# Splitting the work behind the second norm's transposes into three parts, and interleaving the output projection's halves more tightly, in an inference step on one core

## The chip, the cores and the metric

The program runs on one core of one Trainium2 chip. TensorE (PE, with its weight loads shown apart as PEld), VectorE (DVE), ScalarE (ACT), GpSimd (POOL) and SyncE (SP) each have an instruction queue of their own, which they work off in order; semaphores make one engine wait for another. The metric is the device time of one execution in microseconds (us), as the median of several runs. Before the change it is 2565.86 us, the median of 3 runs from 2562.7 to 2570.66.

## The reference

One decoder layer is applied to a prompt of 2048 positions and, with the same weights, to 8 samples of 4 positions (32 rows). All data are fp32, the model width is 1024. Cut to what matters here:

```python
def _layer_prompt(x, ...):
    q, k, v, u, vg = _project(x, norm1_g, w_in)          # RMSNorm, one projection
    ...                                                  # dilated attention -> att, gating unit -> u * gate
    x = x + jnp.concatenate([att, u * gate], axis=-1) @ w_out
    x = x + _swiglu(x, norm2_g, w_gate, w_up, w_down)

def _swiglu(x, g, w_gate, w_up, w_down):                 # D_FF = 2816
    h = _rmsnorm(x, g)
    return (jax.nn.silu(h @ w_gate) * (h @ w_up)) @ w_down
```

The change concerns the stretch from `@ w_out` to the first products with `w_gate` and `w_up`.

## The kernel before

Every fp32 operand of a matmul is split into a high part (rounded to TensorE's fp32r type) and a low part, the rest; a product is then three matmuls: high by high, high by low, low by high. Splitting is therefore a large part of the work beside TensorE: ACT makes the high part by a copy, and DVE or POOL subtracts it from the value to give the low part (`split_sb`, whose two instructions stand on lines 134 and 137 wherever it is called).

The 2048 positions are 16 token tiles of 128. The second half of the program works through them in three blocks: tiles 0 to 5, 6 to 11, and 12 to 15 together with the 32 sample rows. Within a block the tiles are numbered from 0; in the last block the sample rows are number 4. Each block has an opening, and then the SwiGLU, which takes the hidden width in 22 steps of 128 columns (f = 0 to 21).

The opening. The output projection of a tile is made in two halves of 512 columns: an "open" unit for the first half (`o0`, `o1`, ... in the table of the order) and a "second" unit for the second half (`s0`, `s1`, ...). A unit consists of two half units of 12 matmuls. After each half the result in PSUM is added to the residual in SBUF (L1364); the squares for the second norm are summed on ACT, half by half (L1385, L1391) or for the whole row (L1398); then comes the chain of the norm: L1373 and L1374 on DVE, a square root on ACT (L1375), four tiny DVE steps that refine the reciprocal root (L141 to L145), and L1406, which writes the normed tile xn (a buffer named pair; xns for the sample rows). `norm2_c` transposes xn by 8 matmuls on TensorE (L1420) into two PSUM tiles (ps_t). From those, three ACT copies (L1435, L1436, L1438) and six DVE subtractions (the low parts L1437 and L1440, and the four differences L1428 to L1431) give the operands of a Winograd product: seven products instead of eight stand for a two by two block product. The differences t1 to t4 lie in two buffers named zn and are split in two calls of `split_sb`, with the high parts on ACT and the low parts on POOL. Below, T0 to T5 are the transposes of tiles 0 to 5, and Ts those of the sample rows.

The SwiGLU's first step. For f = 0 the block's tiles are taken in two units, unit 0 (tiles 0 to 3; in the last block tiles 0 and 1) and unit 1 (the other two tiles), so that the first products can begin before all tiles are normed. A unit has seven products, q0 to q6, each 12 matmuls (L1552 to L1554) whose moving side is 256 columns wide in unit 0 of the first two blocks, 128 in their unit 1, and 136 in both units of the last block, where the sample rows are dealt out over the units. q0 needs the high and low part of the first transposed block (the low part is L1437's), q1 needs the difference t2, split by ACT and POOL. The later steps take the whole block at once (384 columns wide, 272 in the last block).

What sets the order. No scheduler decides it: the program issues the instructions in the order in which the Python code runs, and each engine has its own of them in that order. `tick()` is called once for each half unit or product, and `later(n, fn)` has fn run n ticks later. So the emission of the small work is spread by hand over the units of TensorE. The tables are in `next_block`: the string `work` orders the units, t says at which tick each first half is closed (`first_end`), and the last argument of `second_end`, put_off, says how many ticks after L1406 the tile is transposed.

In blocks 1 and 2 the opening begins while the block before is still ending: its last down products run on TensorE, and `finals` puts the final norm of each of its tiles (L1653 on ACT, L1374, L1375, L141 to L145, L1661 on DVE) in between. The loading and splitting of the second half of w_out falls there too: `half1_split` takes its eight slices two at a time into buffers named woh and wol, with the low parts on DVE or POOL. In the first block alone the even slices' low parts are DVE's. Slices of the activations are split by L1344 (ACT) and L1345 (DVE). Combined sources of the weights (`sources`) are loaded, summed and split on ACT and on DVE or POOL (L1492, L1496).

Of the kernel before, what the change touches and what calls it, by code (L numbers as in the profile page):

```python
# [64 lines left out]
def hymba_step(ctx: ExitStack, tc: tile.TileContext, A: dict, O: dict):  # L65
# [1336 lines left out]
    def norm2_b(B, i, s1, put_off):  # L1402
        n = B.rows[i]
        r = rms_c(s1, n)
        xn = square_tile() if n == P else B.xns
        dve.scalar_tensor_tensor(xn[:n], B.acc[i][:n], r, gain[1][:n], op0=OP.mult, op1=OP.mult)  # L1406
        if n == P:

            later(put_off, norm2_c, B, i, xn)

    def norm2_c(B, i, xn):
# [12 lines left out]
        (t1, t2), (t3, t4) = ((s_[:, 0], s_[:, 1]) for s_ in sums)  # L1424

        def sums_of():
# [4 lines left out]
            dve.tensor_sub(t4, b21, t2)  # L1431

        if n == P:
            at_ = lambda x, j0, j1: x[:, i, j0:j1, :, 0:64]
            act.activation(at_(hi, 0, 1)[:, 0], b11, AF.Copy)  # L1435
            act.activation(t4, b12, AF.Copy)  # L1436
            dve.tensor_sub(at_(lo_, 0, 1)[:, 0], b11, at_(hi, 0, 1)[:, 0].bitcast(F32))  # L1437
            act.activation(at_(hi, 1, 3), pts[1], AF.Copy)  # L1438
            sums_of()
            dve.tensor_sub(at_(lo_, 1, 3), pts[1], at_(hi, 1, 3).bitcast(F32))  # L1440
            for s_, j in zip(sums, (3, 5)):
                split_sb(at_(hi, j, j + 2), at_(lo_, j, j + 2), s_)
        else:
            act.activation(t4, b12, AF.Copy)
            sums_of()
            for j, x in enumerate((b11, b21, b22, t1, t2, t3, t4)):
                at_ = lambda y: y[:, :, j, :, 64:].rearrange("p i k c -> p k i c")
                x = x.rearrange("p k (i c) -> p k i c", i=B.nt)
                split_sb(at_(hi), at_(lo_), x, eng_lo=dve)
# [333 lines left out]
    def first_block(B):  # L1783
# [45 lines left out]
    def next_block(B, downs, finals):  # L1829
# [28 lines left out]
        for part in work.split():  # L1858
            i = int(part[1])
            if part[0] == "s":  # L1860
                second_end(B, i, second_unit(B, i), (2, 2, 2, 2, 1, 2)[i] if not B.last else (2, 2, 1, 3, 2)[i])
# [4 lines left out]
            if B.last and i == 3:  # L1866
# [186 lines left out]
```

## Time and profile before

| what | value |
|---|---|
| time, median of 3 runs | 2565.86 us (2562.7 to 2570.66) |
| the profiled execution | 2577.92 us, span 2576.1 us |
| mean granted TensorE clock in it | 0.978 |
| busy: PE, DVE, ACT, POOL | 2482.0, 1332.2, 1011.4, 1310.3 us |
| the opening of block 0 around its transposes | about 940 to 996 us |
| the opening of block 1 | about 1499 to 1590 us |
| the opening of the last block | about 2090 to 2151 us |
| f = 0 of the last block | about 2151 to 2192 us |

The profiled execution took 12 us longer than the median of the timed ones, and every duration that is read from the trace belongs to it. Times in the trace count from the start of the span. A row of the timeline gives start and duration in us, the engine, the line, the operation, output and inputs with their shape, and in brackets how long the engine had been idle and which instruction's end released it. A row of the waits says which line of an engine waited for what: us in total, times, and the longest. A row of the windows gives for a stretch its length, each engine's busy time with its instructions in parentheses, the granted clock of TensorE as a share of full speed (PEclk), and the DMA engines' load.

### The profile page before, as it was taken

How to read it: one execution, taken by the hardware profiler on the slowest of the kernel's cores; microseconds unless marked ns; L12 is line 12 of the kernel's file. 1: busy time of each engine (PE TensorE's matmuls, PEld its weight loads, DVE VectorE, ACT ScalarE, POOL GpSimd, SP SyncE). 2: the span in 40 equal slices, each digit the busy share in tenths (PEclk: the TensorE clock that was granted, in tenths of full speed). 3: DMA queues.
4: the chain of work that ended last, by engine and by line, in shares of the span. 5: the costliest groups of instructions: out<-in, count | busy, mean ns of one | idle time of the engine just before them, and what ended most of it. 6: DMA issues, size and time to landing. Idle time of an engine off the chain costs nothing. (4 is left out here: it accounts for less than half of the span.)

```text
span 2576.1 us, 38951 instructions
## 1 busy us (share of the span) xinstructions
PE 2482.0 (96%) x14106; PEld 2145.2 (83%) x14106; DVE 1332.2 (52%) x2628; ACT 1011.4 (39%) x2076; POOL 1310.3 (51%) x1012
## 2 busy tenths in 40 slices
PE   8999989999999898999999999999999999999997
PEld 6787776667888678999999978999999978999996
DVE  3349784215777656444444465444444465444445
ACT  5424333325676534232332344323233244344432
POOL 2035552004777627777676635536455343666662
PEclk9999999999999999999999999999999997999998
DMA  7764944685555454556364473635446362655553
GB/s 237 228 209 133 270 141 149 201 256 187 185 164 163 116 181 145 176 165 201 127 213 155 135 221 109 217 128 195 169 151 217 115 209 82 210 204 191 194 187 110
DMA packets 290708, 453.79 MB, mean 176 GB/s; under 512 B 28407, under 2 KB 160680, under 8 KB 285396
## 3 DMA queue, kind: packets, MB, share of 16 engines
q1 hardware_dynamic: 285396, 442.39, 52.9%
q10 hardware_dynamic: 5120, 8.92, 1.3%
q8 instruction: 112, 1.84, 0.3%
q14 instruction: 80, 0.66, 0.1%
HBM read 363.49 MB, written 157.84 MB: 202 GB/s over the span
## 5 line engine op out<-in xcount | busy, mean ns | idle before, releaser
L1496 POOL TENSOR_TENSOR op<-fr,op 128x512 fp32r<-128x512 f32 x385 | 490.2, 1301 | 266.2 <-ACT op L1492 243.5
L1552 PE MATMUL ps_m<-xh,op 128*128 128x384 f32 (+4 forms) x1932 | 622.0, 322 | 0.0
L1553 PE MATMUL ps_m<-xl,op 128*128 128x384 f32 (+4 forms) x1932 | 621.7, 322 | 0.0
L1554 PE MATMUL ps_m<-xh,op 128*128 128x384 f32 (+4 forms) x1932 | 621.0, 321 | 0.0
L1625 PE MATMUL ps_o<-dw,hw 128*128 128x512 f32 x2040 | 491.6, 397 | 4.3 <-DVE acc L1627 4.3
L1625 PEld LDWEIGHTS ps_o<-dw,hw 128*128 128x128 f32 x2040 | 382.0, 188 | 91.2 <-DVE acc L1627 6.1
L1552 PEld LDWEIGHTS ps_m<-xh,op 128*128 128x128 f32 x1932 | 373.8, 193 | 4.5
L1553 PEld LDWEIGHTS ps_m<-xl,op 128*128 128x128 f32 x1932 | 373.5, 193 | 4.1
L1554 PEld LDWEIGHTS ps_m<-xh,op 128*128 128x128 f32 x1932 | 373.9, 194 | 0.0
L1627 DVE TENSOR_TENSOR acc<-acc,ps_o 128x512 f32<-128x512 f32 (+1 forms) x362 | 248.0, 686 | 234.4 <-PE ps_o L1625 234.4
L1592 ACT ACTIVATE ps_t<-zn 128x384 f32<-128x384 f32 (+1 forms) x126 | 58.3, 463 | 526.0 <-DVE zn L1575 416.6
L1492 ACT ACTIVATE op<-fr 128x512 fp32r<-128x512 f32 x396 | 235.6, 626 | 18.2 <-DMA fr<-ab_d 14.9
L137 POOL TENSOR_TENSOR dw<-fd,dw 128x1024 fp32r<-128x1024 f32 x66 | 159.8, 2421 | 123.3 <-ACT dw L134 123.1
L317 PE MATMUL ps_s<-wh,xh 128*128 128x512 f32 x480 | 200.1, 417 | 5.8 <-ACT xh L134 5.6
L318 PE MATMUL ps_s<-wl,xh 128*128 128x512 f32 x480 | 191.4, 399 | 0.0
L319 PE MATMUL ps_s<-wh,xl 128*128 128x512 f32 x480 | 191.1, 398 | 0.0
L1496 POOL TENSOR_TENSOR op<-pair,op 128x512 fp32r<-128x512 f32 x63 | 81.6, 1304 | 124.7 <-ACT op L1492 124.7
L317 PEld LDWEIGHTS ps_s<-wh,xh 128*128 128x128 f32 x480 | 92.9, 194 | 48.4 <-issue 23.2
L1602 ACT ACTIVATE hw<-ps_t 128x384 fp32r<-128x384 f32 (+1 forms) x126 | 56.2, 454 | 177.6 <-DVE ps_t L1598 176.7
L907 POOL CAST sq<-k 128x512 fp32r<-128x512 f32 x32 | 34.1, 1064 | 164.5 <-PE ps_s L318 164.5
L319 PEld LDWEIGHTS ps_s<-wh,xl 128*128 128x128 f32 x480 | 92.5, 193 | 20.8 <-DVE xl L137 0.2
L318 PEld LDWEIGHTS ps_s<-wl,xh 128*128 128x128 f32 x480 | 93.0, 194 | 16.8 <-DVE wl L225 0.5
(452 smaller groups left out, 4199.4 us busy)
## 6 DMA issues: line engine op xcount, KB each, us to landing
fr<-ab_d SPq DMA_DIRECT2D x308, 256.0 KB
fd<-in_w_down_dram SPq DMA_DIRECT2D x66, 512.0 KB
out_ks_dram<-in_cache_k_dram SPq DMA_DIRECT2D x56, 512.0 KB
out_vs_dram<-in_cache_v_dram SPq DMA_DIRECT2D x56, 512.0 KB
ab_d<-fr SPq DMA_DIRECT2D x88, 256.0 KB
raw<-in_w_in_dram SPq DMA_DIRECT2D x72, 256.0 KB
qk_d<-pair SPq DMA_DIRECT2D x64, 256.0 KB
ab_d<-pair SPq DMA_DIRECT2D x63, 256.0 KB
```

The lines of the kernel that those rows point to most:

```text
L137: (eng_lo or pool).tensor_sub(lo, src, hi.bitcast(F32))
L317: pe.matmul(o[j], xh[:, k, :], wh, start=(k == 0), stop=False)
L318: pe.matmul(o[j], xh[:, k, :], wl, start=False, stop=False)
L319: pe.matmul(o[j], xl[:, k, :], wh, start=False, stop=(k == KD - 1))
L1492: act.activation(ops[f, j][0], ab[f][j], AF.Copy)
L1496: (pool if f or j in POOL_LOW else dve).tensor_sub(lo_, ab[f][j], hi.bitcast(F32))
L1552: pe.matmul(out, wh[:, ks], xh[:, :, k], start=(k == 0), stop=False)
L1553: pe.matmul(out, wh[:, ks], xl[:, :, k], start=False, stop=False)
L1554: pe.matmul(out, wl[:, ks], xh[:, :, k], start=False, stop=(k == 3))
L1592: act.activation(g, c, AF.Silu)
L1625: pe.matmul(ps[0:nr], l_, r_[:, cs], start=(z == 0 and y == 0), stop=(z == FC - 1 and y == len(pairs) - 1))
L1627: dve.tensor_add(B.acc[i][0:nr, cs], B.acc[i][0:nr, cs], ps[0:nr])
```

## The change

Nothing is computed otherwise, and the number of instructions stays the same. Three things move.

First, `norm2_c` keeps only the transposes and the three ACT copies. The DVE work goes into `norm2_d`, one tick later, with the four differences first and the two low parts behind them. The splits of the differences go into `norm2_e`, one more tick later; a negative put_off (tile 3 of block 0) puts them right behind `norm2_d`. The sample rows have one copy first, and everything else one tick later.

Second, in blocks 1 and 2 the even slices of the second half of w_out have their low parts on DVE too, and the splits come one to three ticks earlier, at ticks 7 to 10.

Third, the tables are new: in block 1 the second units start one unit earlier (`s0` behind `o1`), and likewise in the last block (`s4` behind `o1`); the sample rows are transposed behind the opening of tile 2 rather than of tile 3; and the put_offs are new.

```diff
-    def norm2_c(B, i, xn):
+    def norm2_c(B, i, xn, fast=False):
...
-        def sums_of():
+        act.activation(t4, b12, AF.Copy)
+        if n == P:
+            at_ = lambda x, j0, j1: x[:, i, j0:j1, :, 0:64]
+            act.activation(at_(hi, 0, 1)[:, 0], b11, AF.Copy)
+            act.activation(at_(hi, 1, 3), pts[1], AF.Copy)
+
+        def norm2_d():
 
             dve.tensor_sub(t1, t4, b11)
             dve.tensor_sub(t3, b22, t4)
             dve.tensor_sub(t2, b22, t1)
             dve.tensor_sub(t4, b21, t2)
-
-        if n == P:
-            at_ = lambda x, j0, j1: x[:, i, j0:j1, :, 0:64]
-            act.activation(at_(hi, 0, 1)[:, 0], b11, AF.Copy)
-            act.activation(t4, b12, AF.Copy)
-            dve.tensor_sub(at_(lo_, 0, 1)[:, 0], b11, at_(hi, 0, 1)[:, 0].bitcast(F32))
-            act.activation(at_(hi, 1, 3), pts[1], AF.Copy)
-            sums_of()
-            dve.tensor_sub(at_(lo_, 1, 3), pts[1], at_(hi, 1, 3).bitcast(F32))
+            if n == P:
+                dve.tensor_sub(at_(lo_, 0, 1)[:, 0], b11, at_(hi, 0, 1)[:, 0].bitcast(F32))
+                dve.tensor_sub(at_(lo_, 1, 3), pts[1], at_(hi, 1, 3).bitcast(F32))
+                if fast:
+                    norm2_e()
+                else:
+                    later(1, norm2_e)
+                return
...
+        def norm2_e():
             for s_, j in zip(sums, (3, 5)):
                 split_sb(at_(hi, j, j + 2), at_(lo_, j, j + 2), s_)
...
+        later(1, norm2_d)
...
-            split_wo(B, 1, s, half1_place, dve if B.b0 == 0 and s % 2 == 0 else None)
+            split_wo(B, 1, s, half1_place, dve if s % 2 == 0 else None)
...
-            second_end(B, i, p, 1 if i < 5 else 2)
+            second_end(B, i, p, {3: -1, 4: 2, 5: 3}[i])
...
-        work, t = (("o0 o1 o2 s0 o3 s1 o4 s2 o5 s3 s4 s5", (12, 13, 15, 18, 22, 26)) if not B.last else
-                   ("o4 o0 o1 o2 s4 s0 s1 o3 s2 s3", (13, 15, 17, 24, 10)))
+        work, t = (("o0 o1 s0 o2 s1 o3 s2 o4 s3 o5 s4 s5", (10, 11, 15, 19, 23, 27)) if not B.last else
+                   ("o4 o0 o1 s4 s0 o2 s1 o3 s2 s3", (13, 15, 19, 23, 10)))
...
-            later((8, 9, 10, 12)[y] + B.last * (y > 0), half1_split, B, 2 * y, 2 * y + 1)
+            later(7 + y, half1_split, B, 2 * y, 2 * y + 1)
...
-                second_end(B, i, second_unit(B, i), (2, 2, 2, 2, 1, 2)[i] if not B.last else (2, 2, 1, 3, 2)[i])
+                second_end(B, i, second_unit(B, i), (2, 2, 2, 2, 2, 3)[i] if not B.last else (2, 2, 2, 3, 2)[i])
...
-            if B.last and i == 3:
+            if B.last and i == 2:
                 norm2_c(B, n - 1, B.xns)
```

Lines behind the edit have moved by a few: the ACT copies are L1428, L1425 and L1429 now, the differences L1433 to L1436, the low parts L1438 and L1439, the weights' splits L1497 and L1501, the products L1557 to L1559, the final norm's last step L1666.

The order of the units and transposes on TensorE, before and now (`c0` and `c1` are the half units of a unit that a transpose divides):

```
block 0 before: ... s1 o5 T1 s3 T2 s4 T3 s5    T4 q0 q1 q2    T5 q3 q4 q5 q6
block 0 now:    ... s1 o5 T1 s3 T2 s4 T3 s5 q0 T4    q1 q2 q3 T5    q4 q5 q6
block 1 before: o0 o1 o2 s0 o3 s1c0 T0 s1c1 o4 s2c0 T1 s2c1 o5 s3c0 T2 s3c1 s4 s5c0 T3 s5c1 T4 q0 q1 q2 T5 q3 ...
block 1 now:    o0 o1 s0 o2 s1c0 T0 s1c1 o3 s2c0 T1 s2c1 o4 s3c0 T2 s3c1 o5 s4c0 T3 s4c1 s5 q0 T4 q1 q2 q3 T5 q4 ...
last, before:   o4 o0 o1 o2 s4 s0 s1 o3c0 T0 o3c1 Ts s2c0 T1 s2c1 s3 T2 q0 q1 q2 q3 T3 q4 ...
last, now:      o4 o0 o1 s4 s0 o2 Ts s1c0 T0 s1c1 o3 s2c0 T1 s2c1 s3 q0 T2 q1 q2 q3 T3 q4 ...
```

How the queues of DVE and ACT change is shown at three places. First, DVE's queue in block 0 around the norm of tile 3 (ps_t_9533 and ps_t_9538 before, ps_t_9529 and ps_t_9534 now, are tile 2's transposes; acc_9356 is tile 3's residual). Before:

```order
L1428 TENSOR_TENSOR zn<-zn,ps_t_9533 128x256
L1429 TENSOR_TENSOR zn<-ps_t_9538,zn 128x256
L1430 TENSOR_TENSOR zn<-ps_t_9538,zn 128x256
L1431 TENSOR_TENSOR zn<-ps_t_9538,zn 128x256
L1440 TENSOR_TENSOR xl_9100<-ps_t_9538,xh_9099 128x512
L1374 TENSOR_SCALAR s_9524<-s_9524 128x1
L1496 TENSOR_TENSOR op<-raw,op 128x512
L141 RECIPROCAL s_9524<-s_9524 128x1
L143 TENSOR_SCALAR s_9524<-s_9524 128x1
L144 TENSOR_SCALAR s_9524<-s_9524 128x1
L145 TENSOR_SCALAR s_9524<-s_9524 128x1
L1406 SCALAR_TENSOR_TENSOR pair<-acc_9356,s_9524,fd 128x1024
```

And now, in the same queue:

```order
L1374 TENSOR_SCALAR s_9520<-s_9520 128x1
L1501 TENSOR_TENSOR op<-raw,op 128x512
L141 RECIPROCAL s_9520<-s_9520 128x1
L143 TENSOR_SCALAR s_9520<-s_9520 128x1
L144 TENSOR_SCALAR s_9520<-s_9520 128x1
L145 TENSOR_SCALAR s_9520<-s_9520 128x1
L1406 SCALAR_TENSOR_TENSOR pair<-acc_9356,s_9520,fd 128x1024
L1433 TENSOR_TENSOR zn<-zn,ps_t_9529 128x256
L1434 TENSOR_TENSOR zn<-ps_t_9534,zn 128x256
L1435 TENSOR_TENSOR zn<-ps_t_9534,zn 128x256
L1436 TENSOR_TENSOR zn<-ps_t_9534,zn 128x256
L1438 TENSOR_TENSOR xl_9100<-ps_t_9529,xh_9099 128x256
```

Tile 2's six subtractions stood ahead of tile 3's norm, and stand behind it now. The same has happened with tile 3's subtractions and tile 4's norm, and with tile 4's and tile 5's.

Second, DVE's queue at the start of block 1 (acc_14442 is the residual of block 1's tile 0, whose first half is added here; acc_9356 is a finished tile of block 0). Before:

```order
L1345 TENSOR_TENSOR xl_14305<-xl_14305,xh_14304 128x1024
L1374 TENSOR_SCALAR s_14479<-s_14479 128x1
L141 RECIPROCAL s_14479<-s_14479 128x1
L143 TENSOR_SCALAR s_14479<-s_14479 128x1
L144 TENSOR_SCALAR s_14479<-s_14479 128x1
L145 TENSOR_SCALAR s_14479<-s_14479 128x1
L1661 SCALAR_TENSOR_TENSOR acc_9356<-acc_9356,s_14479,final_g 128x1024
L1345 TENSOR_TENSOR xl_14305<-xl_14305,xh_14304 128x1024
L1374 TENSOR_SCALAR s_14529<-s_14529 128x1
L1364 TENSOR_TENSOR acc_14442<-acc_14442,ps_t_14465 128x512
```

And now:

```order
L1345 TENSOR_TENSOR xl_14305<-xl_14305,xh_14304 128x1024
L137 TENSOR_TENSOR woh<-fr,woh 128x512
L1374 TENSOR_SCALAR s_14484<-s_14484 128x1
L1364 TENSOR_TENSOR acc_14442<-acc_14442,ps_t_14470 128x512
L137 TENSOR_TENSOR wol<-fr,wol 128x512
L141 RECIPROCAL s_14484<-s_14484 128x1
L143 TENSOR_SCALAR s_14484<-s_14484 128x1
L144 TENSOR_SCALAR s_14484<-s_14484 128x1
L145 TENSOR_SCALAR s_14484<-s_14484 128x1
L1666 SCALAR_TENSOR_TENSOR acc_9356<-acc_9356,s_14484,final_g 128x1024
L1345 TENSOR_TENSOR xl_14305<-xl_14305,xh_14304 128x1024
L1364 TENSOR_TENSOR acc_14496<-acc_14496,ps_t_14520 128x512
```

Four low parts of w_out (two woh, two wol) have come into this queue. Ahead of the add of tile 0's second half stand now those four, with one final norm and one L1345 fewer than before; that L1345 and that final norm stand between the add and tile 0's L1406 now.

Third, ACT's queue in the last block around the transposes of tile 2 (ps_t_20265 and ps_t_20270 before, ps_t_20288 and ps_t_20293 now); L1562, now L1567, copies the result of the first product q0. Before:

```order
L1391 ACTIVATE xh_19613,s_20166<-acc_19965 128x512
L1492 ACTIVATE op<-fr 128x512
L1435 ACTIVATE xh_19613<-ps_t_20265 128x4x64
L1436 ACTIVATE zn<-ps_t_20265 128x256
L1438 ACTIVATE xh_19613<-ps_t_20270 128x8x64
L134 ACTIVATE xh_19613<-zn 128x8x64 x2
L1375 ACTIVATE s_20166<-s_20166 128x1
L1562 ACTIVATE raw<-ps_m_20293 128x136
```

And now:

```order
L1391 ACTIVATE xh_19613,s_20150<-acc_19975 128x512
L1497 ACTIVATE op<-fr 128x512
L1375 ACTIVATE s_20150<-s_20150 128x1
L1567 ACTIVATE raw<-ps_m_20268 128x136
L1497 ACTIVATE op<-fr 128x512
L1425 ACTIVATE zn<-ps_t_20288 128x256
L1428 ACTIVATE xh_19613<-ps_t_20288 128x4x64
L1429 ACTIVATE xh_19613<-ps_t_20293 128x8x64
```

The first product comes ahead of tile 2's transposes now, and tile 3's square root no longer stands behind the splits of tile 2's differences.

More of the change, by code (lines that the diff above doesn't have):

```diff
@@ L1407, in norm2_b @@
         if n == P:
-            later(put_off, norm2_c, B, i, xn)
-    def norm2_c(B, i, xn):
+            later(abs(put_off), norm2_c, B, i, xn, put_off < 0)
+    def norm2_c(B, i, xn, fast=False):
         n = B.rows[i]
@@ L1431, in sums_of @@
             dve.tensor_sub(t4, b21, t2)
[L1433 to L1440 removed]
+            if n == P:
[6 more added lines that the diff above has]
+                return
+            for j, x in enumerate((b11, b21, b22, t1, t2, t3, t4)):
+                to = lambda y: y[:, :, j, :, 64:].rearrange("p i k c -> p k i c")
+                x = x.rearrange("p k (i c) -> p k i c", i=B.nt)
+                split_sb(to(hi), to(lo_), x, eng_lo=dve)
+        def norm2_e():
             for s_, j in zip(sums, (3, 5)):
                 split_sb(at_(hi, j, j + 2), at_(lo_, j, j + 2), s_)
[L1443 to L1449, printed above, removed]
+        later(1, norm2_d)
     ab, ops = {}, {}
```

## The prediction

> **What bounds the kernel.** I read the page first, then TensorE's waits, then the clock by stage.
>
> ```profile
> PE 2482.0 (96%) x14106; PEld 2145.2 (83%) x14106; DVE 1332.2 (52%) x2628; ACT 1011.4 (39%) x2076; POOL 1310.3 (51%) x1012
> ...
> PE ps_t L1420 <- DVE pair L1406: 18.6, 6, 6.2
> ```
>
> TensorE is busy for 96% of the span and the change takes no matmul away. So only TensorE's idle time and its slow clock can be won. Its largest wait is the change's subject: transposes that wait for the normed tile. By block (openings of blocks 0, 1 and last):
>
> ```profile
> PE ps_t L1420 <- DVE pair L1406: 10.6, 3, 6.2
> ...
> PE ps_t L1420 <- DVE pair L1406: 5.6, 2, 3.3
> ...
> PE ps_t L1420 <- DVE pair L1406: 2.4, 1, 2.4
> PE ps_o L1359 <- POOL wol L137: 1.5, 2, 0.9
> ...
> PE ps_o L1358 <- ACT wol L134: 0.3, 1, 0.3
> ```
>
> The clock is in the windows (the next to last column but one):
>
> ```profile
> 940.00:975.00 35.00, 28.76 (x131) 23.34 (x130) 28.19 (x56) 16.76 (x37) 11.95 (x8) 0.90 0.34 115
> 975.00:996.00 21.00, 16.68 (x117) 15.65 (x115) 15.75 (x36) 9.57 (x21) 11.62 (x9) 0.92 0.38 116
> 996.00:1005.00 9.00, 9.00 (x83) 9.00 (x82) 6.18 (x11) 4.08 (x10) 7.03 (x6) 1.00 0.48 177
> ...
> 1565.00:1589.00 24.00, 18.35 (x126) 17.02 (x125) 16.65 (x42) 12.23 (x28) 11.61 (x8) 0.93 0.22 67
> ...
> 2150.00:2160.00 10.00, 10.00 (x54) 10.00 (x55) 7.91 (x18) 6.43 (x14) 5.55 (x4) 0.58 0.16 47
> 2160.00:2192.00 32.00, 32.00 (x150) 32.00 (x151) 8.57 (x30) 11.09 (x28) 12.37 (x10) 0.50 0.38 123
> ```
>
> Time lost to the clock is (1 - PEclk) times the length: at most 3.5 and 1.7 us in block 0 (part of it lies beside idle time), 1.7 in block 1, and 4.2 + 16.0 = 20.2 us in the last block, where the 136-wide products of f = 0 ran at half speed for about 40 us with TensorE busy all the time. Their start follows the last block's 2.4 us wait; the 128-wide products of block 0 (996 to 1005) kept full speed. Of block 1's waits, 5.6 - 3.3 = 2.3 and 3.3 us, the 1.7 us pays for half speed of some 3.4 us, so only one of the two slowed the clock. A wait of 2 to 2.5 us can thus go either way; in the narrow stage what it starts lasts. The most that can be won is 18.6 + 1.8 + 27.1 = 47.5 us.
>
> **Block 0: -3.4 us.** Tile 3's wait of 6.2 us is a queue on DVE:
>
> ```profile
> 962.57 0.42 DVE L1437 TENSOR_TENSOR xl<-ps_t,xh 128x256 fp32r<-128x256 f32 x1 [2.80 <-ACT zn L1436]
> ...
> 964.36 0.68 DVE L1440 TENSOR_TENSOR xl<-ps_t,xh 128x512 fp32r<-128x512 f32 x1
> ...
> 965.01 1.52 DVE L1496 TENSOR_TENSOR op<-raw,op 128x512 fp32r<-128x512 f32 x1
> 966.46 0.15 DVE L141 RECIPROCAL s<-s 128x1 f32<-128x1 f32 x1
> ...
> 967.39 1.34 DVE L1406 SCALAR_TENSOR_TENSOR pair<-acc,s,fd 128x1024 f32<-128x1024 f32 x1
> ...
> 976.64 2.05 DVE L1406 SCALAR_TENSOR_TENSOR pair<-acc,s,fd 128x1024 f32<-128x1024 f32 x1
> ...
> 954.31 1.15 ACT L134 ACTIVATE xh<-zn 128x512 fp32r<-128x512 f32 x2 [2.44 <-DVE zn L1430]
> ...
> 962.43 0.59 ACT L1438 ACTIVATE xh<-ps_t 128x512 fp32r<-128x512 f32 x1
> ```
>
> Tile 2's six subtractions (962.57 to 965.04, 2.5 us) went ahead of tile 3's norm and go behind it now. Not all of it is won: the square root's queue, ACT, has tile 1's postponed pair of L134 (1.15 us) behind tile 2's copies (until 963.0), so the root comes at about 964.2, DVE's small steps start at 964.5 instead of 966.46, and the wait shrinks by 2.0 to 4.2 us. Bounds: 2.5 less, if ACT has those splits done earlier, and nothing less. The waits of tiles 4 and 5 (10.6 - 6.2 = 4.4 us together) go: q0 is ahead of tile 4, and tile 5's norm no longer stands behind tile 4's subtractions. What is late next is q0. It needs tile 3's low part, which stands behind tile 4's L1406 and is the fifth of six instead of the first. By the rows tile 4's adds come at about 969 to 970.6, its L1406 (1.3 to 2.05 us) ends near 976, and five subtractions later it is 977.9; TensorE reaches q0 about 975.2. I take 3 us (bounds 2 and 4). Tile 0's subtractions now follow an add in the queue, which delays tile 1 by up to 2 us: 1. Unit 1's q1 is the fourth: tile 5's splits wait for q4 (its adds stand ahead on DVE) and q5 (ACT). The chain behind T5:
>
> ```profile
> 993.05 0.42 DVE L1572 TENSOR_TENSOR raw<-raw,ps_m 128x256 f32<-128x256 f32 x1 [0.84 <-PE ps_m L1554]
> ...
> 994.47 0.42 DVE L1575 TENSOR_TENSOR raw<-raw,ps_m 128x256 f32<-128x256 f32 x1 [0.47 <-PE ps_m L1554]
> ...
> L137 POOL TENSOR_TENSOR xl<-zn,xh 128x512 fp32r<-128x512 f32 x12 | 17.2, 1454 | 43.1 <-ACT xh L134 43.1
> ```
>
> A product takes 1.42 us. q4, two adds of 0.42, four differences (1.6), ACT's pair and silu (about 1.5) and one low part (1.45) come to 6.8 us; TensorE's three products and unit 1's q0 (12 x 9.0/83 = 1.3 us) take 5.6. That is 1.2 us late, more where POOL and DVE slow each other down: 2 us, bounds 0 and 3. Two of the new waits can slow the clock for 3.4 us each (3.4 us of it in all). Sum: -(10.6 + 5.2) + 4.2 + 3 + 1 + 2 + 2.2 (the clock, of at most 3.4) = -3.4; bounds -8 and +2.
>
> **Block 1: +0.8 us.** The waits of tiles 4 and 5 (5.6) and the clock's 1.7 go, for the same reasons. The price is at the front.
>
> ```profile
> 1500.70 1.22 DVE L1345 TENSOR_TENSOR xl<-xl,xh 128x1024 fp32r<-128x1024 f32 x1
> ...
> 1510.14 2.31 DVE L1345 TENSOR_TENSOR xl<-xl,xh 128x1024 fp32r<-128x1024 f32 x1
> ...
> 1516.43 1.75 DVE L1345 TENSOR_TENSOR xl<-xl,xh 128x1024 fp32r<-128x1024 f32 x1 [0.49 <-ACT xh L1344]
> ...
> 1520.61 1.29 DVE L1661 SCALAR_TENSOR_TENSOR acc<-acc,s,final_g 128x1024 f32<-128x1024 f32 x1
> 1521.96 0.69 DVE L1364 TENSOR_TENSOR acc<-acc,ps_o 128x512 f32<-128x512 f32 x1
> ...
> 1525.14 1.28 DVE L1406 SCALAR_TENSOR_TENSOR pair<-acc,s,fd 128x1024 f32<-128x1024 f32 x1
> ...
> 1503.86 4.02 POOL L137 TENSOR_TENSOR woh<-fr,woh 128x512 fp32r<-128x512 f32 x2 [17.16 <-ACT woh L134]
> ...
> 1530.15 1.03 PE L1420 MATMUL ps_t<-ident,pair 128*128 128x128 f32 x8
> ```
>
> Before, T0 came at 1530.15 with tile 0 normed at 1526.4, 3.7 us early. Now T0 is due one unit of 5.6 us sooner, at 1524.6. The add of 1521.96 was DVE's backlog: it can lose one L1345, one L1661 and its 0.95 us of small steps (4.0 us) and up to 2.7 us of idle gaps, and gets four low parts. Their cost on DVE is not in this stretch; the same form took 0.68 alone (half of L1440's kind) to 1.52 us (the L1496 above), so 2.7 to 6.1. The add comes between 1518 and 1523. From it to the normed tile it was 4.5 us; a first half's add (0.7) leaves, an L1345 and a final norm (1.2 to 1.75, and 2.2) come in: 7.2 to 7.8. T0 waits between 0.6 and 6 us. I take 3.5, nearer the middle since POOL's half of the splits is shorter too, and half of one slow clock window, 0.9. Later: T4 and T5 0.7 together by the same chain, unit 1's q0 1 and its q1 2. Sum: -7.3 + 3.5 + 0.9 + 0.7 + 3 = +0.8; bounds -5 and +8.
>
> **Last block: -7.6 us.** Away go 2.4 (T2 comes behind q0), 1.8 (the wol splits are earlier and shared by two engines) and 20.2 us of clock, together 24.4.
>
> ```profile
> 2123.62 1.27 DVE L1406 SCALAR_TENSOR_TENSOR xns<-acc,s,fd 32x1024 f32<-32x1024 f32 x1
> ...
> 2134.49 0.68 PE L1420 MATMUL ps_t<-ident,xns 32*128 32x32 f32 x8
> ```
>
> The sample rows' transposes came 9.6 us after their norm. Now two units and T0 (12.2 us) and the 1.8 us of waits are gone from ahead of them: due at 2120.5. Their norm moves too, since s4 is a unit earlier, but DVE has the same backlog as in block 1: wait 0.5 to 4, I take 3. T0 0.8, one slow window 1.7, waits at q0 or T3 1, unit 1's q0 and q1 2. Then the clock in the narrow stage: at half speed a product takes 12 x 32/150 = 2.56 us, at full speed 1.3 x 136/128 = 1.38 (an estimate from the 128-wide rows), so a unit of seven loses 8.3 us. Nothing idles for 2 us directly ahead of unit 0 any more, so I let unit 0 run at full speed; unit 1 begins with two waits, and I let its clock fall: 8.3. Sum: -24.4 + 3 + 0.8 + 1.7 + 1 + 2 + 8.3 = -7.6.
>
> A rule speaks against that last term. The Trainium skill ("TensorE: Matmul & The Clock Gate", section "What's actually happening") lets full speed return after one busy window of about 3.4 us; section "Seeing it yourself" adds that the monitor has been seen stuck for over 50 us. The trace's 40 us at half speed beside a busy TensorE contradict the first and look like the second; by the rule alone unit 1 would lose 1.7 us in place of 8.3.
>
> **Sum.** -3.4 + 0.8 - 7.6 = -10.2 us: the profiled span would be 2565.9, and with the same difference the median 2565.86 - 10 = **2556 us**.
>
> **Rivals.**
> The narrow stage never falls to half speed, or leaves it at once (that rule, as a mechanism here): 8.3 less in the last block, and if T0 of block 1 hardly waits, 4.4 less there: -22.9, **2543 us**. For it: the 128-wide stages kept 1.00. Against: the waits ahead of unit 1.
> Slower: the late low part of the unit's last tile makes q1 wait in unit 1 of all three blocks, and where the wait reaches about 2 us the clock falls and stays down for the rest of the unit. Six products at 128 wide cost about 7 us each in blocks 0 and 1, and in the last block unit 0 falls as well: -3.4 + 7 + 0.8 + 7 - 7.6 + 8.3 = +12, **2578 us**. For it: POOL's low parts are two ticks later everywhere, and 40 us show that narrow products don't reopen the clock. Against: the chain is only 1.2 us late by the bare rows.
> No change: another wait ahead of T2 or q1 closes the clock over the last block's whole stage as before, or the timed runs never had that stage (they are 12 us shorter than the profiled one, and no view says where). Then the last block gives -4.2 + 8.5 = +4.3, in all +1.7: **2567 us**.
>
> **How the numbers follow.** Changes under 0.3% (7.7 us) can't be told from none here. My forecast has 0.38; with its own range of 2548 to 2565 it is faster in 0.25 and within the bound in 0.13. The fast rival 0.18, all faster. The slow one 0.23 (0.20 slower, 0.03 the same). No change 0.21 (0.16 the same, 0.04 slower, 0.01 faster). Faster 0.44, same 0.32, slower 0.24. The cases lie on both sides, so the range covers most of the outer two: 2541 to 2581.
>
> **What would show it.** Right: T3 of block 0 waits about 4 us and q0 behind it about 3; T4 and T5 don't wait; T0 of block 1 and the sample's transposes are new waits of 1 to 6 us; the clock is 1.00 in the last block's unit 0. Wrong: no wait at T0 (POOL and DVE shared the splits faster), clock 0.50 over both narrow units (then about 2567), or below 1.00 in the 128-wide stages (then 2578).

## The result and the profile after

The changed kernel takes 2595.78 us (median of 4 runs, 2591.97 to 2602.78), against 2568.26 us for the kernel before in the runs shared with it: a ratio of 1.0111 with a 95% interval of 1.0077 to 1.0145. It is slower, and above the range that was forecast. Its profiled execution took 2599.12 us (span 2597.3), 21.2 us more than the profiled execution of before.

The engines' busy time on the page of the changed kernel:

```profile
PE 2494.8 (96%) x14106; PEld 2157.6 (83%) x14106; DVE 1333.0 (51%) x2636; ACT 1009.1 (39%) x2076; POOL 1296.8 (50%) x1004
```

TensorE's waits over its whole span (us in total, times, longest), those at the transposes and first products:

```profile
PE ps_t L1420 <- DVE xl L1438: 8.4, 4, 2.7
...
PE ps_t L1420 <- DVE pair L1406: 4.8, 1, 4.8
...
PE ps_m L1558 <- DVE xl L1438: 3.7, 3, 2.1
...
PE ps_t L1420 <- DVE xns L1406: 2.4, 1, 2.4
PE ps_t L1420 <- DVE xl L137: 2.3, 1, 2.3
PE ps_m L1558 <- POOL xl L137: 2.0, 2, 1.0
...
PE ps_t L1420 <- ACT xh L134: 1.0, 1, 1.0
...
PE ps_m L1557 <- ACT xh L134: 0.9, 2, 0.5
```

TensorE's 18.6 us of transposes waiting for a normed tile (L1406) have shrunk to 4.8, and 2.4 for the sample rows, as the edit's order suggests. But TensorE's busy time went up by 12.8 us with the same 14106 matmuls, so they ran slower; and other waits took the old one's place: transposes that wait for the low part of the tile before (L1438, which reads the PSUM tiles that the transposes want to write), and first products that wait for L1438, L134 or L137. Summed over these rows, waits on this work are 25.5 us. The clock by stage (windows; PEclk is the number after the parentheses of POOL):

```profile
975.00:994.00 19.00, 16.90 (x115) 15.82 (x114) 14.59 (x33) 9.47 (x21) 9.84 (x7) 0.91 0.46 149
994.00:1014.00 20.00, 17.72 (x90) 17.29 (x89) 9.12 (x18) 5.77 (x14) 13.99 (x11) 0.60 0.21 79
...
1588.00:1601.00 13.00, 11.16 (x95) 10.80 (x94) 10.65 (x25) 7.58 (x17) 9.28 (x6) 1.00 0.40 123
1601.00:1621.00 20.00, 17.72 (x89) 17.29 (x88) 9.16 (x20) 6.39 (x15) 10.40 (x8) 0.62 0.42 145
...
2173.00:2182.00 9.00, 7.33 (x61) 6.96 (x59) 8.41 (x19) 6.28 (x14) 7.43 (x4) 1.00 0.27 87
2182.00:2212.00 30.00, 29.71 (x140) 29.62 (x141) 10.74 (x34) 10.70 (x28) 12.68 (x10) 0.51 0.38 123
```

Unit 1 of blocks 0 and 1 (994 to 1014, 1601 to 1621), whose 128-wide products had the full clock before, ran at 0.60 and 0.62, and the last block's narrow stage at 0.51, as before. The row of unit 1 of block 1 before the change, beside the prediction's 1.00 for block 0 (996 to 1005):

```profile
1589.00:1599.00 10.00, 10.00 (x91) 10.00 (x90) 4.37 (x13) 5.17 (x12) 6.60 (x6) 1.00 0.55 184
```

Where the 21 us came from follows from the start times of the same matmuls in the two traces:

| first matmul of | before, us | after, us | ahead or behind | this stretch |
|---|---|---|---|---|
| unit 1, block 0 | 995.69 | 994.41 | -1.3 | |
| third product of f = 1, block 0 | 1009.25 | 1020.30 | +11.0 | unit 1 and its end: +12.3 |
| the opening of block 1 | 1499.39 | 1509.63 | +10.2 | steps between: -0.8 |
| unit 1, block 1 | 1589.21 | 1601.16 | +11.9 | opening of block 1: +1.7 |
| third product of f = 1, block 1 | 1602.77 | 1625.73 | +23.0 | unit 1 and its end: +11.0 |
| the opening of the last block | 2090.14 | 2113.11 | +23.0 | steps between: 0.0 |
| fourth product of f = 1, last block | 2194.42 | 2215.66 | +21.2 | last block: -1.7 |

So the openings gained little, and the two units 1 lost 23.3 us. What happens at their head is shown by TensorE's first rows that waited there (timeline; in brackets the idle time and what ended it), in block 0 and in block 1:

```profile
995.45 0.33 PE L1558 MATMUL ps_m<-xl,op 128*128 128x128 f32 x1 [0.82 <-DVE xl L1438]
997.35 0.33 PE L1557 MATMUL ps_m<-xh,op 128*128 128x128 f32 x1 [0.45 <-ACT xh L134]
998.69 0.47 PE L1558 MATMUL ps_m<-xl,op 128*128 128x128 f32 x1 [1.01 <-POOL xl L137]
...
1602.19 0.33 PE L1558 MATMUL ps_m<-xl,op 128*128 128x128 f32 x1 [0.81 <-DVE xl L1438]
1604.09 0.33 PE L1557 MATMUL ps_m<-xh,op 128*128 128x128 f32 x1 [0.45 <-ACT xh L134]
1605.44 0.33 PE L1558 MATMUL ps_m<-xl,op 128*128 128x128 f32 x1 [1.02 <-POOL xl L137]
```

q0 waits for the low part of the unit's last tile, q1 for a high part and then for a low part: 2.28 us of idle time within 4 us, in three pieces of at most 1.02. From there the clock is half, and full again only 4.7 and 2.4 us after the first 384-wide product (windows of the two stretches at half clock):

```profile
998.10:1018.60 20.50, 19.91 (x86) 19.91 (x87) 8.24 (x14) 6.32 (x16) 17.78 (x15) 0.50 0.24 90
1605.70:1622.80 17.10, 17.10 (x79) 17.10 (x79) 5.80 (x13) 6.10 (x14) 8.82 (x7) 0.50 0.54 184
```

Half of each stretch and the 2.28 us of waits make 12.5 and 10.8 us, against the 12.3 and 11.0 of the table.

### The profile page after: what moved, and what is told of

The parts are those of the page before. It is cut to its first block, busy times and chain, and to the rows that moved or that the text cites. A ratio compares the mean times of both kernels' runs of the same rounds, so it can differ in the third digit from the quotient of the medians.

```text
span 2597.3 us, 38974 instructions
## 1 busy us (share of the span) xinstructions
PE 2494.8 (96%) x14106; PEld 2157.6 (83%) x14106; DVE 1333.0 (51%) x2636; ACT 1009.1 (39%) x2076; POOL 1296.8 (50%) x1004
## 3 DMA queue, kind: packets, MB, share of 16 engines
q8 instruction: 112, 1.84, 0.3%
## 5 line engine op out<-in xcount | busy, mean ns | idle before, releaser
L1557 PE MATMUL ps_m<-xh,op 128*128 128x384 f32 (+4 forms) x1932 | 627.2, 325 | 0.9 <-ACT xh L134 0.9
L1501 POOL TENSOR_TENSOR op<-fr,op 128x512 fp32r<-128x512 f32 x385 | 490.9, 1307 | 271.5 <-ACT op L1497 246.2
L1559 PE MATMUL ps_m<-xh,op 128*128 128x384 f32 (+4 forms) x1932 | 626.3, 324 | 0.0
L1557 PEld LDWEIGHTS ps_m<-xh,op 128*128 128x128 f32 x1932 | 378.6, 196 | 5.8 <-ACT xh L134 1.2
L1559 PEld LDWEIGHTS ps_m<-xh,op 128*128 128x128 f32 x1932 | 378.9, 196 | 0.0
L1497 ACT ACTIVATE op<-fr 128x512 fp32r<-128x512 f32 x396 | 236.1, 626 | 18.0 <-DMA fr<-ab_d 12.0
L137 POOL TENSOR_TENSOR dw<-fd,dw 128x1024 fp32r<-128x1024 f32 x66 | 159.9, 2422 | 123.9 <-ACT dw L134 123.9
L1501 POOL TENSOR_TENSOR op<-pair,op 128x512 fp32r<-128x512 f32 x63 | 81.3, 1298 | 132.1 <-ACT op L1497 132.1
L317 PEld LDWEIGHTS ps_s<-wh,xh 128*128 128x128 f32 x480 | 92.5, 193 | 48.5 <-issue 23.3
L137 POOL TENSOR_TENSOR xl<-zn,xh 128x512 fp32r<-128x512 f32 x32 | 48.6, 1541 | 136.8 <-ACT xh L134 99.8
```

The lines of the kernel that those rows point to most:

```text
L137: (eng_lo or pool).tensor_sub(lo, src, hi.bitcast(F32))
L317: pe.matmul(o[j], xh[:, k, :], wh, start=(k == 0), stop=False)
L1497: act.activation(ops[f, j][0], ab[f][j], AF.Copy)
L1501: (pool if f or j in POOL_LOW else dve).tensor_sub(lo_, ab[f][j], hi.bitcast(F32))
L1557: pe.matmul(out, wh[:, ks], xh[:, :, k], start=(k == 0), stop=False)
L1559: pe.matmul(out, wl[:, ks], xh[:, :, k], start=False, stop=(k == 3))
```

## The experiments

The theory after the result (the clock theory): idle time at the head of a narrow unit lowers TensorE's clock, and products 128 or 136 columns wide do not bring it back, so the unit's whole length is paid for a 2 us wait. The rival (the wait theory): the time went into the waits themselves and into slowed side engines. Medians are given with the ratio to the kernel before from the shared runs. The kernel before took 2568.26 to 2571.56 us in the different sets of runs, so a difference between medians of two sets is good to some 3 us.

### Spare matmuls at the head of unit 1

```diff
 def product(B, u, q):
     f, a, b = u["f"], u["a"], u["b"]
     n = (b - a) * B.w
+    if f == 0 and a and q < 2 and not B.last:
+        ps_ = ps_o()
+        for _ in range((3, 6)[q]):
+            pe.matmul(ps_, ops[f, q][0][:, 0:P], ops[f, q][0], start=True, stop=True)
```

> The changed kernel with 3 and 6 spare matmuls (512 wide, results read by nobody) put ahead of unit 1's q0 and q1 in the first two blocks, to fill the 0.8 and 1.5 us for which TensorE idles there; the waits for VectorE, ScalarE and GpSimd stay as they are. Clock theory (idle time at the head of a narrow unit lowers TensorE's clock, and narrow products do not bring it back): both units 1 run at clock 1.00, 9 to 12 us less per block, in all 18 to 24 us less than the changed kernel, 2572 to 2578. Wait theory (the time went into the new waits and into slowed side engines): nothing changes, 2593 to 2600.

Measured: 2577.05 us, ratio 1.0028 (1.0016 to 1.0040), 18.7 us less than the changed kernel. The waits for the side engines are as late as they were; only TensorE no longer idles through them, and both units 1 kept the full clock (windows of this kernel around unit 1 in block 0, in block 1 in two rows, and of the last block's narrow stage):

```profile
993.50:1008.00 14.50, 14.09 (x112) 13.27 (x111) 10.55 (x21) 5.94 (x14) 10.46 (x9) 1.00 0.27 99
1590.00:1602.00 12.00, 11.60 (x89) 10.59 (x88) 9.60 (x18) 5.89 (x14) 6.47 (x5) 1.00 0.24 82
1600.00:1612.00 12.00, 12.00 (x94) 12.00 (x94) 6.96 (x14) 7.04 (x16) 9.44 (x8) 1.00 0.72 246
...
2168.00:2197.00 29.00, 28.74 (x139) 28.59 (x140) 10.73 (x34) 10.24 (x28) 12.70 (x10) 0.53 0.37 126
```

More work for TensorE won back some two thirds of the loss. The wait theory can't give that.

### The undivided work for the tiles of unit 1

```diff
 def norm2_c(B, i, xn, fast=False):
+    if (4 if B.nt == 6 else 2) <= i < B.nt:
+        return norm2_whole(B, i, xn)        # norm2_c as it was before
```

> The changed kernel with the undivided work behind the transposes for the tiles of unit 1 alone (tiles 4 and 5, in the last block 2 and 3); all tables and the splits of w_out stay changed. Clock theory: unit 1 no longer waits, both 128-wide units at clock 1.00, and tile 3's transposes of the last block no longer wait for tile 2's PSUM tiles; 2563 to 2575, of which the waits themselves are 6 to 7 us. Wait theory: only those 6 to 7 us, 2587 to 2591.

Measured: 2575.57 us, ratio 1.0022 (1.0007 to 1.0038). Unit 1 no longer waits, and the last block's narrow stage still fell: it had a wait of 2.95 us ahead of tile 3's transposes and 30.7 us at half clock behind it. The time is at the upper end of what the clock theory gave, 20.2 us less than the changed kernel.

### The undivided work for all tiles

```diff
-    def norm2_c ... norm2_d ... norm2_e        # divided
+    def norm2_c(B, i, xn, fast=False): ...     # as before, in one piece
```

> The changed kernel with the undivided work behind the transposes for all tiles and the sample rows: the tables and the w_out splits alone. If the division is what costs the time (by way of the waits ahead of unit 1 and of the transposes that wait for the tile before), this is as fast as the kernel with the division left out for unit 1 alone or faster: 2565 to 2577. If the tables cost the time, it stays above 2585.

Measured: 2572.97 us, ratio 1.0009 (0.9992 to 1.0025): no difference from before that can be told. So of the three parts of the change it is the division that costs the time, 22.8 us. The tables and the w_out splits alone bring nothing: TensorE's waits of this kernel in the openings (us in total, times, longest) are

```profile
PE ps_t L1420 <- DVE pair L1406: 19.4, 5, 6.2
PE ps_o L1625 <- DVE acc L1627: 2.9, 3, 2.0
PE ps_t L1420 <- DVE xns L1406: 2.4, 1, 2.4
PE ps_t L1420 <- DVE xl L137: 1.7, 2, 1.3
```

19.4 us for normed tiles, against 18.6 before: what T4 of blocks 0 and 1 (3.3 us) and T2 of the last block (2.4) no longer wait, and T5 of blocks 0 and 1 wait less (1.8), is taken by T0 of block 1 (4.8) and T3 of the last block (3.5). The division with the tables of before was not tried: there, the next transposes are issued ahead of the work that frees their PSUM tiles.

### The splits of w_out as before

```diff
-            split_wo(B, 1, s, half1_place, dve if s % 2 == 0 else None)
+            split_wo(B, 1, s, half1_place, dve if B.b0 == 0 and s % 2 == 0 else None)
...
-            later(7 + y, half1_split, B, 2 * y, 2 * y + 1)
+            later((8, 9, 10, 12)[y] + B.last * (y > 0), half1_split, B, 2 * y, 2 * y + 1)
```

> The changed kernel with w_out's second half split as before: low parts on GpSimd alone in blocks 1 and 2, and at the later ticks. If VectorE's four extra low parts make T0 of block 1 wait (4.8 us, and 3.4 us at half clock), that wait shrinks to 1 to 3 us, but s0 and s4 may wait for the splits: 2590 to 2596, so 0 to 6 us less than the changed kernel. If the wait is the older backlog (final norms and L1345), it stays at 4 to 6 us and s0 waits on top: 2596 to 2602.

Measured: 2597.35 us, ratio 1.0092 (1.0063 to 1.0121), 1.6 us above the changed kernel's own median, which is no difference that can be told. T0 of block 1 no longer waits at all, and s0 waits for its weights in its place (waits of this kernel from 1480 to 1560 us):

```profile
PE ps_o L1630 <- DVE acc L1632: 2.0, 2, 1.7
PE ps_o L1353 <- ACT wol L134: 1.8, 1, 1.8
PE ps_o L1354 <- POOL wol L137: 1.0, 1, 1.0
PE ps_o L1354 <- POOL woh L137: 0.5, 1, 0.5
```

Neither expectation had both halves right. TensorE now waits 3.3 us for s0's weights ahead of T0, so of T0's 4.8 us this run puts only the other 1.5 down to VectorE's four low parts; and the earlier s0 can't do without them.

### One thing late in the kernel before

```diff
-            for s_, j in zip(sums, (3, 5)):
-                split_sb(at_(hi, j, j + 2), at_(lo_, j, j + 2), s_)
+            def norm2_e():
+                for s_, j in zip(sums, (3, 5)):
+                    split_sb(at_(hi, j, j + 2), at_(lo_, j, j + 2), s_)
+            if i == 5:
+                later(4, norm2_e)
+            else:
+                norm2_e()
```

> The kernel before with one thing late: the splits of tile 5's differences come four ticks later in blocks 0 and 1, so that q1 of unit 1 waits some 2 to 3 us there. Clock theory: clock 0.50 through both units 1, 2 to 3 us of wait and 8 to 10 us of slow clock per block, 20 to 26 us more than before, 2586 to 2594. Wait theory: only the wait, 4 to 6 us more, 2570 to 2574.

Measured: 2588.85 us, ratio 1.0065 (1.0040 to 1.0090), single runs between 2568.26 and 2598.01. In the profiled execution q1 waits in block 0 for

```profile
PE ps_m L1558 <- POOL xl L137: 1.0, 1, 1.0
PE ps_m L1557 <- ACT xh L134: 0.7, 1, 0.7
```

and the units 1 of blocks 0 and 1 behind such waits have, in the windows,

```profile
995.00:1016.00 21.00, 20.23 (x95) 20.24 (x96) 4.69 (x11) 7.41 (x16) 19.50 (x16) 0.59 0.23 87
1596.00:1617.00 21.00, 20.26 (x95) 20.26 (x96) 3.09 (x11) 7.38 (x16) 13.12 (x11) 0.59 0.46 155
```

The wait was smaller than expected, 1.7 us, and still the clock went to half for 17 us each time. Two waits of 1.7 us make the kernel before some 19 us slower by the medians. The single runs are 30 us apart, and the clock accounts for it: the shortest execution had a mean granted clock of 0.982, the longest 0.971 (worked out below, under "Timed and profiled"). So such a wait seems not to lower the clock every time; no trace of a shorter execution shows the place.

### One size changed: three tiles in each unit

```diff
-        part = 4 if B.nt == 6 else 2
+        part = 3 if B.nt == 6 else 2
```

> The changed kernel with one size changed: in blocks 0 and 1 the first step's tiles are taken three and three, so unit 1's products are 192 wide in place of 128 (unit 0's 192 in place of 256). If the clock comes back only where products are wide enough, and 192 is, a fall at unit 1's head lasts one window of 3.4 us: 10 to 20 us less than the changed kernel, 2576 to 2586. If 192 is too narrow as well, the slow stretches are as long or longer: 2593 to 2610.

Measured: 2583.55 us, ratio 1.0036 (1.0021 to 1.0051), 12.2 us less than the changed kernel. The waits at the head of unit 1 are still there (0.88 and 0.99 us in block 0), the clock falls, and with 192-wide products it comes back by itself (windows in blocks 0 and 1):

```profile
999.00:1003.00 4.00, 3.39 (x16) 3.39 (x17) 3.76 (x4) 1.10 (x3) 3.92 (x4) 0.57 0.00 0
1003.00:1007.00 4.00, 4.00 (x23) 4.00 (x23) 0.35 (x1) 1.74 (x4) 3.90 (x4) 0.58 0.65 244
1007.00:1011.00 4.00, 4.00 (x37) 4.00 (x37) 1.87 (x5) 1.04 (x3) 4.00 (x4) 1.00 0.40 150
1600.00:1604.00 4.00, 3.88 (x20) 3.88 (x21) 2.25 (x4) 1.62 (x4) 3.87 (x4) 0.57 0.00 0
1604.00:1608.00 4.00, 4.00 (x39) 4.00 (x38) 1.39 (x4) 1.93 (x4) 2.31 (x3) 1.00 0.81 262
```

6.8 us at half clock in block 0 and 3.4 in block 1, against 20.5 and 17.1 with 128-wide products.

### Spare matmuls in the last block of the kernel before

```diff
 def norm2_c(B, i, xn):
     ...
     hi, lo_ = B.ops
+    if B.last and i == 2:                  # next kernel: tile 3 too, with 9
+        ps_ = ps_o()
+        for _ in range(10):
+            pe.matmul(ps_, ops[0, 0][0][:, 0:P], ops[0, 0][0], start=True, stop=True)
```

> The kernel before with ten spare 512-wide matmuls (2.3 us) ahead of tile 2's transposes in the last block, where TensorE idles for 2.4 us and the clock is then 0.50 for 41 us. Clock theory: the narrow stage of the last block runs at 1.00, 15 to 20 us less than before, 2546 to 2553. Wait theory, or if the timed runs never had that slow stage: within 3 us of before.

Measured: 2566.93 us, ratio 0.9980 (0.9961 to 1.0000), single runs from 2552.12 to 2575.96. The forecast 15 to 20 us are missing in the median; the two shortest executions, 2552.12 and 2557.13, had a mean granted clock of 0.987, the others 0.980 to 0.982. The profiled execution shows why: with tile 2's gap filled, products ran at full clock and so reached tile 3's transposes before tile 3 was normed; that wait lowered the clock for the rest of the stage (the wait of this kernel from 2140 to 2160 us):

```profile
PE ps_t L1424 <- DVE pair L1406: 1.8, 1, 1.8
```

The window behind it:

```profile
2152.00:2184.00 32.00, 31.93 (x153) 31.96 (x154) 9.72 (x33) 11.51 (x29) 15.17 (x12) 0.52 0.38 124
```

Filling that one too:

> The kernel before with spare 512-wide matmuls ahead of tile 2's (ten) and of tile 3's transposes (nine) in the last block. With tile 2's gap filled alone, tile 3's wait of 1.8 us lowered the clock instead, for 30.7 us. Clock theory: with both filled the whole narrow stage runs at 1.00, 15 to 20 us less than before, 2550 to 2555. Wait theory: within 3 us of before.

Measured: 2556.42 us, ratio 0.9927 (0.9905 to 0.9949). The stage now runs at full clock:

```profile
2147.00:2175.00 28.00, 27.83 (x232) 26.85 (x231) 18.88 (x50) 17.10 (x42) 17.50 (x13) 1.00 0.49 161
```

### The changed kernel with its narrow stages filled one after the other

The edit of unit 1's head above, with nine spare matmuls ahead of tile 3's transposes in the last block:

> The changed kernel with spare matmuls at the head of unit 1 in blocks 0 and 1 (three and six) and ahead of tile 3's transposes in the last block (nine, where it waits 2.0 us and the clock is then 0.50 for 27 to 31 us). Clock theory: all narrow units at 1.00, so a further 12 to 16 us less than with unit 1's filling alone, 2561 to 2566: the changed kernel without its clock losses in the narrow units would be a few us faster than before. If the waits and the front of block 1 matter more, 2570 to 2577.

Measured: 2576.67 us, ratio 1.0030 (1.0020 to 1.0041), not less than with unit 1 of blocks 0 and 1 alone. The expected gain failed for the reason just seen: the next waits in the last block, at the head of its unit 1, took over, and the stage behind them ran at half clock (waits of this kernel from 2150 to 2180 us, and the window from 2170).

```profile
PE ps_m L1566 <- POOL xl L137: 1.1, 1, 1.1
PE ps_m L1566 <- DVE xl L1442: 0.8, 1, 0.8
```

```profile
2170.00:2192.00 22.00, 20.99 (x100) 20.99 (x101) 7.02 (x18) 8.25 (x23) 12.76 (x10) 0.53 0.36 120
```

With those filled as well (the condition `not B.last` left out):

> The changed kernel with spare matmuls ahead of unit 1's q0 and q1 in all three blocks and ahead of tile 3's transposes in the last block. With tile 3's wait filled alone, the waits at the head of the last block's unit 1 lowered the clock in its place, for 20.5 us. Clock theory: no narrow unit below 1.00 any more, 8 to 11 us less than with that kernel, 2564 to 2569. The kernel before, with its narrow stage held at 1.00, took 2556; if the rest of the difference is the front of block 1 (4.8 us of wait and 3.4 us at half speed beside it) and the sample rows' transposes (2.4 us), this kernel stays 7 to 12 us above that. If the clock is not the cause, 2575.

Measured: 2566.53 us, ratio 0.9989 (0.9980 to 0.9998). The last block's stage is at full clock now:

```profile
2155.00:2200.00 45.00, 44.69 (x334) 42.05 (x333) 26.39 (x64) 24.10 (x57) 35.98 (x27) 1.00 0.63 205
```

By the medians the clock in narrow stages costs the changed kernel 18.7 us in blocks 0 and 1 and 10 us in the last, 29 in all. With its narrow stages held at full clock, it is still about 10 us behind the kernel before with the last block's gaps filled (2556.42). The likely reason, which no run isolates, is that its new waits, T0 of block 1 (4.8 us, with 6.8 us at half clock around it) and the sample rows' transposes (2.4) first, are worth more than those it removed.

### A faster version

> The kernel before with spare matmuls in all six waits ahead of transposes (block 0: tiles 3 and 5, block 1: tiles 4 and 5, last block: tiles 2 and 3). Clock theory: beside the last block's 15 us, four slow windows of 3.4 to 6.8 us go, each worth half its length, 5 to 8 us in all, but the waits themselves stay: 2548 to 2553. Wait theory: as with the last block's two alone, 2556.

```diff
 # the kernel before, in norm2_c, spare matmuls ahead of these (block's first tile, tile):
+    {(0, 3): 18, (0, 5): 12, (6, 4): 8, (6, 5): 8, (12, 2): 10, (12, 3): 9}
```

Measured: 2559.86 us, ratio 0.9955 (0.9936 to 0.9974), not better than the last block's two alone. In block 0 the spare matmuls themselves had to wait 7.3 us, for the PSUM bank that tile 4's add (L1364) was still to read, and came behind the wait that they were to fill:

```profile
PE ps_o L1418 <- DVE acc L1364: 7.3, 1, 7.3
```

Then with the put_off tables of the change, which put q0 ahead of the next tile's transposes:

```diff
-            second_end(B, i, p, 1 if i < 5 else 2)
+            second_end(B, i, p, i - 2)
...
-                second_end(B, i, second_unit(B, i), (2, 2, 2, 2, 1, 2)[i] if not B.last else (2, 2, 1, 3, 2)[i])
+                second_end(B, i, second_unit(B, i), (2, 2, 2, 2, 2, 3)[i] if not B.last else (2, 2, 2, 3, 2)[i])
...
+    {(0, 3): 18, (0, 5): 10, (6, 5): 8, (12, 3): 12}      # spare matmuls; next kernel: without (0, 3)
```

> The kernel before with the changed put_off tables only (q0 ahead of the next tile's transposes, tile 5 one product later) and the undivided work, its unit order and w_out splits as before, and spare matmuls in the waits that are left (block 0: tiles 3 and 5, block 1: tile 5, last block: tile 3). The late tables take 2 to 3 us of wait away in each block; with the clock held up: 2543 to 2552. If the tables bring nothing, 2550 to 2556.

Measured: 2553.9 us, ratio 0.9933 (0.9908 to 0.9958). And without the one that waits for its bank:

> The kernel before with the changed put_off tables and spare matmuls ahead of tile 5's transposes in blocks 0 and 1 and of tile 3's in the last block, but none ahead of tile 3's in block 0, where they had to wait for their PSUM bank and cost about 4 us. Clock theory and waits together: 2547 to 2552, about 1% less than the changed kernel's partner before. If that bank wait was hidden anyway: 2553 to 2556.

Measured: 2547.68 us, ratio 0.9908 (0.9891 to 0.9925). It is the fastest of all, 22 us below the kernel before in the runs shared with it and 48 below the changed one. Its narrow stage in the last block:

```profile
2138.00:2165.00 27.00, 26.74 (x220) 25.80 (x219) 17.34 (x49) 16.94 (x43) 18.33 (x13) 1.00 0.47 157
```

## Why the prediction was wrong

The forecast was 2556 us and the measured time 2595.78. The waits were sized about right in sum (24.2 us forecast, 25.5 in the rows above); the step that failed is the one that let unit 1's waits in blocks 0 and 1 cost only themselves. Between the forecast's -10.2 us and the +21.2 of the two traces lie 31.4: 18.3 in the two units 1 (23.3 against 5 of waits), 5.9 in the last block, 4.1 in block 0 ahead of unit 1 (-1.3 against -5.4), 3.9 in the opening of block 1, and -0.8 in the steps between.

**Block 0.** Four waits were forecast, 4.2 (T3), 3 (q0), 1 (T1) and 2 us (unit 1): 10.2. Measured were 2.69 (T3), 2.10 (q0), 1.05 (T1), 2.28 (unit 1) and one that was not forecast, 1.89 (T2): 10.0. But T3's cause was misread. DVE's and TensorE's rows of the changed kernel:

```profile
970.22 0.41 DVE L1438 TENSOR_TENSOR xl<-ps_t,xh 128x256 fp32r<-128x256 f32 x1
970.55 0.68 DVE L1439 TENSOR_TENSOR xl<-ps_t,xh 128x512 fp32r<-128x512 f32 x1
...
970.78 1.92 PE L1420 MATMUL ps_t<-ident,pair 128*128 128x128 f32 x8 [2.69 <-DVE xl L1438]
```

T3 waits for tile 2's low parts, the last readers of the PSUM tiles that it overwrites, and so does T2 for tile 1's. The row ends its wait at the end of L1438, the first of the two. The prediction moved tile 2's subtractions behind tile 3's norm on DVE and counted only the gain; that the same subtractions hold the transposes' only pair of PSUM tiles was not in it. The clock's part of the opening was put at 2.2 us; the three windows of 3.4 us that are seen there (960.6, 970.8 and 981.1) cost 1.7 each.

**Unit 1 of blocks 0 and 1.** A wait of 2 us was forecast for both, with 1 us more in block 1, and 2.28 came in each. Its consequence was given to a rival, with a chance of 0.23 and 7 us per unit. Measured: 12.3 and 11.0 us in the traces with the waits in them, 9.4 us per unit by the filled kernel. The row of 1.00 in 996 to 1005 said only that narrow products keep a clock that is up; the row beside it, 40 us at 0.50, said that they don't raise one that is down. Both were in the text, and in the sum the step from there to a fall that lasts to the end of the unit was made for the last block alone. The rival's condition was a wait of about 2 us; against it stood that the chain is late by 1.2 us, while the sum itself took 2. The longest single gap is 1.02 us, and three gaps within 4 us were enough.

**Block 1's front.** T0's wait was put at 3.5 us between 0.6 and 6, and is 4.81, for the reason given: the add of tile 0's second half came at 1531.35, with PE done with s0 at 1526.6, behind four low parts, three final norms and three L1345. The half clock beside it was 6.8 us long where half of one window had been counted. T4 does not wait, T5 waits 1.84 us (0.7 for both was forecast). The opening as a whole came out at +1.7 us up to unit 1, against -2.2 without unit 1's 3 us.

**Last block.** The sample rows' transposes wait 2.36 us (3 forecast). T0 waits 2.35 where 0.8 was forecast, again for the PSUM tiles: the sample rows' low parts (L137) still read them. The clock fell in unit 0, at tile 3's wait of 1.96 us, which is a PSUM wait too (T3 starts at 2182.29, and the first of tile 2's two low parts ends at 2181.73 plus 0.41), and not at unit 1: 30.7 us at half clock cost 15.4 us, where 8.3 were counted for seven products. -7.6 us was forecast, -1.7 measured.

**The rule of the Trainium skill** named in the prediction ("TensorE: Matmul & The Clock Gate", section "What's actually happening": full speed after one busy window of about 3.4 us) fits the products of 384 and 272 columns, behind whose start the full clock came after 2.4 to 5.2 us, and, within 3.4 to 6.8 us, those of 192. It does not fit those of 128 and 136, which stayed at half speed for 17 to 41 us with TensorE busy: that was right in the prediction, and should have been applied to all three blocks. The remark of the Trainium skill that the prediction set beside it (same page, section "Seeing it yourself") is about a quarter of the rate ("K=1/4"); the stretches here are at half, and end with the first wider products.

**The rivals.** The slow one (2578) was the right mechanism and 18 us too small. By its terms block 0 is +3.6 and block 1 +7.8, where the table has +11.0 and +12.7: it priced six products of a unit and left out the head of f = 1, and it kept the gains forecast for the openings of blocks 0 and 1 (5.4 and 2.2 us; 1.3 and -1.7 came). In the last block its +0.7 was near (-1.7). The fast one (a narrow stage that recovers at once) is refuted by the stretches of 17.1 and 20.5 us at 0.50. The one of no change had the last block's stage at half clock right, and nothing of the units 1.

**Timed and profiled.** The changed kernel is 27.5 us slower in the timed runs and 21.2 in the profiled ones. The mean granted clock is on record for single executions too, and (1 - clock) times the span is what the clock takes (rounded, to some 1.3 us). The four executions of the changed kernel lose 65 to 70 us in this way, 31 of the kernel before 46 to 62; the medians are 69 and 51, and without this part the spans are 2526 and 2518 us. So about 17 us of the slowdown are clock and about 9 are not. The profiled execution of the kernel before lost 57 us, more than its median, which is why the two traces are only 21.2 apart. That the clock differs so between executions of one kernel shows best in the kernel before with one thing late: 46 us in its shortest execution, 75 in its longest, and without this part all ten spans lie between 2519.5 and 2525.9 us. What decides it in an execution is not shown.

## What to carry to other kernels

Before a stage of narrow matmuls, count TensorE's idle time at its head by what the clock does behind it: here 1.7 to 2.4 us of waits cost 9 to 20 us. Moving work behind a transpose later also moves the moment at which its PSUM tiles come free, so the next transposes and the last tile's products must be followed in the same working. Where a gap can't be closed, spare matmuls in it keep the clock up, if their own output bank is free, and if the next gap behind is filled as well.

## What the runs showed of the hardware

Products of 128 or 136 columns that follow one another without idle time keep TensorE at full clock (128: 1.00 from 996 to 1005 us before; 136: 1.00 from 2147 to 2175 with both of the last block's gaps filled) and do not bring it back from half (0.50 from 2160 to 2192 before, and in the two stretches of 20.5 and 17.1 us after); products of 192 columns do within 3.4 to 6.8 us. Every stretch at half clock in these traces, but for the one at the program's end, is a multiple of about 3.4 us long: 3.4, 6.8, 10.2, 17.1, 20.5, 27.3, 30.7, 41.0. Idle time need not be in one piece to start one: 0.7 and 1.0 us within 2 us were enough in the kernel before with one thing late. A filled gap can turn the next, harmless one into the cause, since at full clock TensorE reaches it earlier: with tile 2's filled, tile 3's transposes waited 1.8 us, and 30.7 us at half clock followed.
